# Norm ahead of the first layer's first FFN sweep, left half: four additions of squares on GpSimd instead of VectorE

## The chip, the cores and the metric

The kernel runs on one core of one Trainium2 chip. A core has a matrix engine (TensorE, PE in the rows; PEld are its weight loads), a vector engine (VectorE, DVE), an activation engine (ScalarE, ACT), a general engine (GpSimd, POOL), and a queue processor that only issues transfers here (SyncE, SP). Each engine executes its own list of instructions strictly in the order in which it was written out; instructions wait for other engines through semaphores. Transfers between device memory and the on-chip memory (SBUF) are carried by 16 DMA engines. The metric is the time of one execution in device microseconds (us), as the median of several runs.

## The reference, cut to what matters

The program is a diffusion backbone with two layers, 1024 channels, 1024 latent tokens and 256 context tokens. Layer 0 mixes tokens with a convolution, layer 1 with attention; behind each stands a SwiGLU feed-forward network (FFN). Around each part stand RMS norms. The part in question is the norm between the convolution and the FFN of layer 0:

```python
def rmsnorm(x, g):
    xf = x.astype(jnp.float32)
    y = xf * lax.rsqrt(jnp.mean(xf * xf, axis=-1, keepdims=True) + EPS)
    return (y * g.astype(jnp.float32)).astype(x.dtype)

x = x + g_x * rmsnorm(yx, norm_g[i, 1])
fx = rmsnorm(x, norm_g[i, 2]) * (1.0 + scf_x) + shf_x
x = x + gf_x * rmsnorm(swiglu(fx, ffn_w1[i], ffn_w3[i], ffn_w2[i]), norm_g[i, 3])
```

For `fx`, the squares of the new `x` have to be summed over all 1024 channels of a token before the first channel of that token can be scaled.

## The kernel before

**Layout.** Channels lie on the 128 partitions, so an activation is eight tiles `k = 0..7` of 128 channels by some number of tokens. The tokens are cut into three pieces: C (256 context tokens), L (the left 512 latent tokens) and R (the right 512). Each float32 operand of a matrix product is split into a rounded high part and the remainder, and each product is three matmuls: high by high, high by low, low by high (`mm3`, `mm3s`; L172 to L174 and L183 to L185, whose third has the weight's low part).

**Weights.** `wload` brings 512 KB of weights into one of two raw buffers (in the rows of the order `wr_73` and `wr_74`, in the profile `wr`) over SP's queue, ACT rounds it to `wh` (L144), and DVE subtracts to get `wl` (L148). SP may issue the next load into a raw buffer only when L148 has read it.

**The norm in question.** `post_pre` runs once for each piece. Its first part is `post`: for each tile DVE multiplies (L693) and adds the residual (L696), which gives the new `x` of the tile. Then `sink(k)` is called: `sq_acc` has ACT square the tile (L387 for the first, straight into the accumulator `acc`; L390 for the others, into one of four scratch buffers `sb`) and adds the square to `acc` (L391), and POOL issues the store of the tile to device memory (`x1d`, L710). Behind the eight tiles, `stat` has PE sum `acc` over the partitions (L365), DVE work out the reciprocal root in some 13 small instructions (L370, L343 to L351), and PE spread the result over the partitions (L379). Last, `apply` makes the FFN's input out of it, with a high part from ACT (L399 on DVE, then L404) and a low part from DVE (L405).

**What runs around it.** The pieces' `post_pre` for C and L is called, then `pw2` for R, which is the convolution's last product, and then the FFN's first sweep over C and L together (the second sweep is over R). R's `post_pre` is queued as background work of the first sweep; its first step has POOL issue four loads of 512 KB into the buffer `HR` (L685), which L's residual occupied before. The first weights of the sweep, `w1` and `w3` of `ft = 0`, are both needed at its first product, and C's products come ahead of L's.

**What sets the order.** The code is written as one program; a scheduler puts the instructions of each engine into a fixed order when the kernel is built, by its own estimate of when their inputs are ready and by the priorities that `later` gives. The order is fixed from then on, so an instruction whose input is late holds up everything behind it on its engine. Moving a few instructions can thereby change the order of others.

**Names in the rows.** `T_3535` is L's `x`, `T_3893` the FFN's input for C, `T_4028` and `T_4029` its high and low part for L, `T_3501` with `HS` the input of R's `pw2`. The profile leaves the numbers out.

Of the kernel before, what the change touches and what calls it, by code (L numbers as in the profile page):

```python
# [18 lines left out]
CTX = 256  # L19
# [27 lines left out]
def segs_of(c0, c1):  # L47
    out = []
    if c0 < CTX:
        out.append((0, min(c1, CTX) - c0, 1))  # L50
    if c1 > CTX:
        out.append((max(c0, CTX) - c0, c1 - c0, 0))
    return out


class Kern:
# [645 lines left out]
    def post_pre(self, l, y, yacc, xsrc, xdst, c0, c1, dcol, xtag, ftags, box):  # L702
        nc = self.nc
        n = c1 - c0
        segs = segs_of(c0, c1)
        acc = self.acc(n)

        def sink(k):
            self.sq_acc(acc, y[:, k, :], k)
            nc.gpsimd.dma_start(xdst[:, k, c0 - dcol:c1 - dcol], y[:, k, :])  # L710
        yield from self.post(l, 1, y, yacc, xsrc, c0, segs, sink, xtag)
        pb = self.stat(acc, n)
        yield self.pace
        hi, lo = self.halves(*ftags, n)
        box.append((hi, lo))
        for k in range(KT):
            self.apply(y[:, k, :], pb, l, 2, segs, hi, lo, k)
            yield self.pace
# [1005 lines left out]
```

## Time and profile before

| | |
|---|---|
| median of three runs | 2931.11 us (2930.49 to 2935.78) |
| profiled execution, its own time | 2934.98 us |
| its span, first to last instruction | 2933.2 us |
| mean granted TensorE clock | 0.987 |
| L's `post`, `stat` and `apply` on DVE | about 497 to 535 us of the span |
| DVE busy | 2160.1 us (74%) |
| ACT busy | 1334.4 us (45%) |
| POOL busy | 228.6 us (8%), 381 instructions |

An engine's busy time says nothing of where it was waited for; that is read from rows in order of time, in which the idle time ahead of an instruction stands at its end in brackets, with the instruction that ended it. A row with several instructions (x2, x3) gives the time from the first one's start to the last one's end. Rows of matmuls overlap, so the pace of PE is the distance between two starts.

### The profile page before, as it was taken

Reading aid. Unit: us, or ns where it says so; the run is one execution under the profiler, and the core shown is the slowest. Engines: PE = TensorE matmul, PEld = TensorE weight load, DVE = VectorE, ACT = ScalarE, POOL = GpSimd, SP = SyncE. Lnnn points to the kernel's source line nnn. Section 1 sums busy time; section 2 is a strip of 40 time slices with the busy share of each in tenths; the row PEclk is TensorE's granted clock in tenths of the full one; section 3 lists DMA queues with packets and bytes.
Section 4 is the critical chain, followed back from the end, with each engine's and each line's share of the span. In section 5 each row is a group of like instructions: output and inputs, shape, how many; then the busy total and the mean of one; then the engine's idle time right before and its main releaser. Section 6 shows DMA issues by size and latency. Waiting matters only on the chain.

```text
span 2933.2 us, 42735 instructions
## 1 busy us (share of the span) xinstructions
PE 2848.9 (97%) x16462; PEld 2446.5 (83%) x16462; DVE 2160.1 (74%) x3742; ACT 1334.4 (45%) x2229; POOL 228.6 (8%) x381
## 2 busy tenths in 40 slices
PE   8999989999999999999999999989999999999998
PEld 5888877888888889989888787767777778889997
DVE  6887788856556378877786899786666666786777
ACT  5212155432222245544444688645555543444444
POOL 0000001011022001000111111110000000010000
PEclk9999989999999999999999999999999999999999
DMA  6443443434356224333345211322222143353332
GB/s 249 133 127 99 111 136 137 139 116 148 104 171 209 64 78 167 108 103 111 119 160 166 89 46 46 101 83 81 65 74 83 60 151 97 109 171 102 105 97 77
DMA packets 131756, 336.58 MB, mean 115 GB/s; under 512 B 31329, under 2 KB 52865, under 8 KB 130657
## 3 DMA queue, kind: packets, MB, share of 16 engines
q1 hardware_dynamic: 78016, 222.33, 24.2%
q0 software_dynamic: 29344, 103.83, 10.8%
q10 hardware_dynamic: 24192, 7.70, 1.1%
q8 instruction: 129, 2.11, 0.3%
q14 instruction: 75, 0.61, 0.1%
HBM read 289.50 MB, written 38.93 MB: 112 GB/s over the span
## 4 chain that ended last, share of the span: by engine, by line
PE 86%; DVE 8%; issue 2%; ACT 2%; DMA 2%; ACTq 0%; SPq 0%; POOL 0%; DVEq 0%; POOLq 0%
PE ps L172 15%; PE ps L173 15%; PE ps L174 15%; PE ps L875 4%; PE ps L877 4%; PE ps L876 4%; PE ps L1116 4%; PE ps L1134 4%; PE ps L1140 2%; PE ps L1141 2%; PE ps L454 2%; PE ps L455 2%; PE ps L456 2%; PE ps L185 1%; PE ps L183 1%
## 5 line engine op out<-in xcount | busy, mean ns | idle before, releaser
L172 PE MATMUL ps<-T,wh 128*128 128x512 f32 (+1 forms) x1360 | 503.5, 371 | 0.6 <-DVE sm L839 0.4
L174 PE MATMUL ps<-T,wl 128*128 128x512 f32 (+1 forms) x1360 | 501.2, 369 | 2.0 <-DVE wl L148 2.0
L173 PE MATMUL ps<-T,wh 128*128 128x512 f32 (+1 forms) x1312 | 482.8, 368 | 0.0
L144 ACT CAST wh<-wr 128x1024 fp32r<-128x1024 f32 (+1 forms) x217 | 225.0, 1037 | 426.3 <-PE ps L173 311.2
L148 DVE TENSOR_TENSOR wl<-wr,wh 128x1024 fp32r<-128x1024 f32 (+1 forms) x217 | 261.9, 1207 | 174.7 <-ACT wh L144 173.4
L875 PE MATMUL ps<-T,wh 128*128 128x256 f32 x1092 | 310.5, 285 | 5.0 <-ACT wh L161 4.5
L876 PE MATMUL ps<-T,wh 128*128 128x256 f32 x1092 | 306.4, 281 | 0.0
L877 PE MATMUL ps<-T,wl 128*128 128x256 f32 x1092 | 305.4, 281 | 0.2 <-DVE wl L164 0.2
L1138 DVE TENSOR_TENSOR T<-ps,T 128x512 fp32r<-128x512 f32 x320 | 216.9, 687 | 108.4 <-ACT T L1137 107.7
L172 PEld LDWEIGHTS ps<-T,wh 128*128 128x128 f32 x1360 | 258.4, 190 | 43.1 <-ACT T L1506 1.7
L174 PEld LDWEIGHTS ps<-T,wl 128*128 128x128 f32 x1360 | 258.6, 190 | 42.5 <-DVE wl L148 2.2
L173 PEld LDWEIGHTS ps<-T,wh 128*128 128x128 f32 x1312 | 249.2, 190 | 37.7 <-DVE T L164 0.7
L1137 ACT CAST T<-ps 128x512 fp32r<-128x512 f32 x320 | 185.9, 585 | 191.5 <-PE ps L1134 177.6
L173 PE MATMUL ps<-HS,wh 128*128 128x512 f32 x656 | 257.9, 393 | 0.0
L172 PE MATMUL ps<-HS,wh 128*128 128x512 f32 x608 | 238.4, 392 | 0.9 <-ACT wh L144 0.9
L174 PE MATMUL ps<-HS,wl 128*128 128x512 f32 x608 | 237.4, 391 | 0.0
L875 PEld LDWEIGHTS ps<-T,wh 128*128 128x128 f32 x1092 | 206.1, 189 | 11.2 <-ACT wh L161 6.7
L876 PEld LDWEIGHTS ps<-T,wh 128*128 128x128 f32 x1092 | 206.6, 189 | 0.5
L877 PEld LDWEIGHTS ps<-T,wl 128*128 128x128 f32 x1092 | 206.1, 189 | 0.6 <-DVE wl L164 0.4
L1134 PE MATMUL ps<-cst,T 128*128 128x128 f32 x1100 | 189.5, 275 | 3.1 <-DVE T L1138 3.1
L1122 DVE TENSOR_SCALAR_CACHE_REDUCE T<-ps,rq 128x1280 f32<-128x1280 f32 x110 | 170.1, 1546 | 27.9 <-PE ps L1116 22.2
L1134 PEld LDWEIGHTS ps<-cst,T 128*128 128x128 f32 x1100 | 132.8, 141 | 49.2 <-DVE T L1138 30.2
(378 smaller groups left out, 6197.4 us busy)
## 6 DMA issues: line engine op xcount, KB each, us to landing
wr<-in_w SPq DMA_DIRECT2D x170, 512.0 KB, 3.6
wr<-in_pw SPq DMA_DIRECT2D x35, 512.0 KB, 3.5
HV<-in_wmodT POOLq DMA_DIRECT2D x56, 256.0 KB, 4.2
q<-in_wmodT POOLq DMA_DIRECT2D x56, 256.0 KB, 3.8
KB<-in_w SPq DMA_DIRECT2D x24, 512.0 KB, 3.6
HR<-in_w SPq DMA_DIRECT2D x23, 512.0 KB, 3.8
q<-in_w SPq DMA_DIRECT2D x23, 512.0 KB, 4.1
q<-qsd POOLq DMA_DIRECT2D x32, 256.0 KB, 3.4
```

The source lines that it names most:

```text
L144: nc.scalar.copy(hi, raw)
L148: nc.vector.tensor_tensor(lo, raw, hi.bitcast(F32), op=ALU.subtract)
L172: nc.tensor.matmul(out[:, :n], lhsT=wh, rhs=xh, start=k == 0, stop=False)
L173: nc.tensor.matmul(out[:, :n], lhsT=wh, rhs=xl, start=False, stop=False)
L174: nc.tensor.matmul(out[:, :n], lhsT=wl, rhs=xh, start=False, stop=k == nk - 1)
L875: nc.tensor.matmul(out, lhsT=wh, rhs=bh, start=first and k == 0, stop=False, **skip)
L876: nc.tensor.matmul(out, lhsT=wh, rhs=bl, start=False, stop=False, **skip)
L877: nc.tensor.matmul(out, lhsT=wl, rhs=bh, start=False, stop=k == 3, **skip)
L1122: nc.vector.tensor_scalar(out=pt, in0=sc, scalar1=rq[:, h:h + 1], scalar2=None, op0=ALU.mult, op1=ALU.min, accum_out=mn)
L1134: nc.tensor.transpose(tp[:, h * P:(h + 1) * P], Ps[h][:, j * P:(j + 1) * P], c["ident"])
L1137: nc.scalar.copy(ph, tp)
L1138: nc.vector.tensor_tensor(pl, tp, ph.bitcast(F32), op=ALU.subtract)
```

## The change

`post_pre` hands `sq_acc` an engine: for L (`c0 == CTX`) and tiles below 5 it is GpSimd. Tile 0 has no addition, so four are moved, those of tiles 1 to 4; the additions of tiles 5, 6 and 7 stay on DVE, and so do all seven of C and of R. Nothing else is edited.

```diff
         def sink(k):
-            self.sq_acc(acc, y[:, k, :], k)
+            self.sq_acc(acc, y[:, k, :], k, nc.gpsimd if c0 == CTX and k < 5 else None)
             nc.gpsimd.dma_start(xdst[:, k, c0 - dcol:c1 - dcol], y[:, k, :])
```

The scheduler's order changes with it. On DVE, this is the end of L's `post` before; `wr_73` holds the last weights of R's `pw2`, and `wr_74` the FFN's first `w1`:

```order
L693 SCALAR_TENSOR_TENSOR T_3535<-T_3535,col_2955,ps 128x512 x2
L391 TENSOR_TENSOR acc<-acc,sb 128x512
L696 TENSOR_TENSOR T_3535<-T_3535,HR 128x512 x2
L148 TENSOR_TENSOR wl<-wr_73,wh 128x1024
L391 TENSOR_TENSOR acc<-acc,sb 128x512
L148 TENSOR_TENSOR wl<-wr_74,wh 128x1024
L391 TENSOR_TENSOR acc<-acc,sb 128x512
L370 TENSOR_SCALAR nv<-ps 128x4
```

And this is the same place after the change, where the second `wr_73` is the FFN's first `w3`, and the second `wr_74` the `w1` of its next step:

```order
L693 SCALAR_TENSOR_TENSOR T_3535<-T_3535,col_2955,ps 128x512 x2
L696 TENSOR_TENSOR T_3535<-T_3535,HR 128x512 x2
L148 TENSOR_TENSOR wl<-wr_73,wh 128x1024
L148 TENSOR_TENSOR wl<-wr_74,wh 128x1024
L391 TENSOR_TENSOR acc<-acc,sb 128x512 x2
L148 TENSOR_TENSOR wl<-wr_73,wh 128x1024
L391 TENSOR_TENSOR acc<-acc,sb 128x512
L148 TENSOR_TENSOR wl<-wr_74,wh 128x1024
L370 TENSOR_SCALAR nv<-ps 128x4
```

Five additions stood ahead of the first L148 (the last of them is shown), now none does; and the two L148 of the next loads, which stood behind the first dozen instructions of the root, now stand ahead of L370.

On POOL, the difference at L's stores and the loads for R behind them (`ISA` sets GpSimd up for the additions and stood further back in the program before):

```order
-L710 DMA x1d<-T_3535 128x512 x8
+L710 DMA x1d<-T_3535 128x512 x2
+L391 ISA
+L391 TENSOR_TENSOR acc<-acc,sb 128x512
+L710 DMA x1d<-T_3535 128x512
+L391 TENSOR_TENSOR acc<-acc,sb 128x512
+L710 DMA x1d<-T_3535 128x512
+L391 TENSOR_TENSOR acc<-acc,sb 128x512
+L710 DMA x1d<-T_3535 128x512
+L391 TENSOR_TENSOR acc<-acc,sb 128x512
+L710 DMA x1d<-T_3535 128x512 x3
 L685 DMA HR<-in_xT 128x2x512 x4
```

The additions stand between the stores, and the four loads behind the last of either.

On PE, the difference among C's products of the first sweep, at the place where L379 stood:

```order
+L185 MATMUL ps<-T_3893,wl 128x256
 L184 MATMUL ps<-T_3893,wh 128x256
 L185 MATMUL ps<-T_3893,wl 128x256
-L379 MATMUL ps<-cst,nr 128x128 x4
+L183 MATMUL ps<-T_3893,wh 128x256
+L184 MATMUL ps<-T_3893,wh 128x256
+L365 MATMUL ps<-cst,acc 128x1 x4
 L185 MATMUL ps<-T_3893,wl 128x256
```

L365 moved back from among R's `pw2` to here, behind 11 of C's 48 products with the first `w1` and `w3`; L379 stands 25 of them further on, with the last 12 behind it. Ten products of C with the next `w1` now stand ahead of L's first low-part product, and all 22 products that are left of R's `pw2` stand ahead of C's first, of which two stood in front of them before.

## The prediction

> **What bounds the kernel now.** The page first. PE is busy for 97% of the span, so only time in which PE waits, or runs slowly, can be won:
>
> ```profile
> PE 2848.9 (97%) x16462; PEld 2446.5 (83%) x16462; DVE 2160.1 (74%) x3742; ACT 1334.4 (45%) x2229; POOL 228.6 (8%) x381
> PE 86%; DVE 8%; issue 2%; ACT 2%; DMA 2%; ACTq 0%; SPq 0%; POOL 0%; DVEq 0%; POOLq 0%
> ```
>
> Shares over the whole span don't say what four additions are worth, so the next view is PE in order of time where L's norm runs, about 497 to 541 us. PE waits there three times:
>
> ```profile
> 509.27 0.40 PE L173 MATMUL ps<-HS,wh 128*128 128x512 f32 x1
> 509.51 0.28 PE L183 MATMUL ps<-T,wh 128*128 128x256 f32 x1
> 509.63 0.28 PE L184 MATMUL ps<-T,wh 128*128 128x256 f32 x1
> 511.89 0.50 PE L174 MATMUL ps<-T,wl 128*128 128x512 f32 x1 [1.98 <-DVE wl L148]
> ...
> 526.54 0.50 PE L184 MATMUL ps<-T,wh 128*128 128x512 f32 x1 [0.36 <-DVE T L405]
> ...
> 540.33 1.05 PE L365 MATMUL ps<-cst,acc 128*128 128x1 f32 x8 [0.54 <-DVE acc L391]
> ```
>
> The distances of the starts also give PE's pace: 0.23 us for a product 512 wide, 0.12 for one 256 wide. The first wait has a second price, in the table by stretches (the eighth figure of a row, behind the five engines' busy times, is the granted clock):
>
> ```profile
> 510.00:512.00 2.00, 0.11 (x1) 0.11 (x2) 2.00 (x4) 1.23 (x2) 1.55 (x3) 1.00 0.25 98
> 512.00:516.00 4.00, 4.00 (x11) 3.14 (x12) 2.17 (x3) 0.22 (x1) 2.41 (x4) 0.57 0.94 297
> 516.00:520.00 4.00, 4.00 (x25) 3.46 (x24) 2.61 (x13) 0.83 (x1) 0.00 (x0) 1.00 1.01 387
> 540.00:545.00 5.00, 4.67 (x27) 4.14 (x28) 4.73 (x16) 0.79 (x2) 0.00 (x0) 1.00 0.46 116
> ```
>
> After the wait of 1.98 us PE has a clock of 0.57 for 4 us, which loses 4 x 0.43 = 1.7 us; after the wait of 0.54 it keeps 1.00. All that can be won here is 1.98 + 1.7 + 0.36 + 0.54 = 4.6 us, 0.16% of the time. A measurement of this kernel tells about 0.2%, 5.9 us, from no change.
>
> **DVE's side.** PE's first wait is for the first L148 of the order shown above. DVE in order of time, from the first addition on:
>
> ```profile
> 501.19 0.69 DVE L391 TENSOR_TENSOR acc<-acc,sb 128x512 f32<-128x512 f32 x1
> 501.79 1.29 DVE L696 TENSOR_TENSOR T<-T,HR 128x512 f32<-128x512 f32 x2
> ...
> 510.61 1.22 DVE L148 TENSOR_TENSOR wl<-wr,wh 128x1024 fp32r<-128x1024 f32 x1
> 511.75 0.68 DVE L391 TENSOR_TENSOR acc<-acc,sb 128x512 f32<-128x512 f32 x1
> 512.35 1.22 DVE L148 TENSOR_TENSOR wl<-wr,wh 128x1024 fp32r<-128x1024 f32 x1
> ...
> 517.09 0.16 DVE L370 TENSOR_SCALAR nv<-ps 128x4 f32<-128x4 f32 x1 [2.92 <-PE ps L365]
> ...
> 519.07 0.16 DVE L350 TENSOR_TENSOR nq<-nq,nh 128x4 f32<-128x4 f32 x1
> ...
> 522.62 1.22 DVE L148 TENSOR_TENSOR wl<-wr,wh 128x1024 fp32r<-128x1024 f32 x1 [2.17 <-ACT wh L144]
> 523.76 2.06 DVE L399 SCALAR_TENSOR_TENSOR sb<-T,col,ps 128x512 f32<-128x512 f32 x3
> 525.74 2.07 DVE L405 SCALAR_TENSOR_TENSOR T<-sb,mod,T 128x512 fp32r<-128x512 f32 x3
> ```
>
> From start to start an addition costs DVE 0.60 us (501.19 to 501.79) and an L148 1.14 (510.61 to 511.75). Five additions stand ahead of 510.61: 3.0 us, of which four go and the fifth moves behind.
>
> **What GpSimd takes, and takes back.** The trace has the same addition on POOL at another place, the norm of layer 1:
>
> ```profile
> 1432.63 1.22 DVE L148 TENSOR_TENSOR wl<-q,wh 128x1024 fp32r<-128x1024 f32 x1
> 1435.68 1.92 DVE L405 SCALAR_TENSOR_TENSOR T<-sb,mod,T 128x512 fp32r<-128x512 f32 x2
> 1439.47 1.34 DVE L405 SCALAR_TENSOR_TENSOR T<-sb,mod,T 128x512 fp32r<-128x512 f32 x1
> ...
> 1432.76 2.25 POOL L391 TENSOR_TENSOR acc<-acc,sb 128x512 f32<-128x512 f32 x1 [6.11 <-ACT sb L390]
> ...
> 1438.97 1.30 POOL L391 TENSOR_TENSOR acc<-acc,sb 128x512 f32<-128x512 f32 x1 [2.59 <-ACT sb L390]
> ```
>
> Undisturbed it takes 1.30 us. It doesn't run beside every DVE instruction: the one at 1432.76, started 0.13 us after an L148, takes 2.25, about what was left of the L148 more. And L405 at 1439.47, which takes 0.69 without POOL (2.07 for three), takes 1.34 beside the addition that began at 1438.97: it was held until about 1440.1, 1.1 us after the addition's start. L148 and L405 have two inputs in SBUF; so has L696, the residual's addition that DVE runs throughout L's `post`. L693, with one of its two from PSUM, I count as free of it, like L399, since all the lengthened rows are of the other kind. The Trainium skill, page "SBUF — State Buffer", section "Who interferes with whom", states this as a rule: a VectorE instruction with two SBUF inputs and a GpSimd instruction that reads SBUF exclude each other, and the one issued first keeps the other out to its end. It speaks against the change; by it nothing but the order of starts decides, and all four additions could hold VectorE in full.
>
> I follow the order through. L693 and L696 alternate in pairs, 1.32 and 1.20 us. The square of tile 1 is ready at 501.2, just as the second pair of L696 would start: a full hold of 1.1. The square of tile 2 comes while a pair of L693 runs, and its addition reaches 0.1 into the next L696. The third has a pair of L693 to itself: nothing. The fourth falls on the last pair of L696, or on the L148 behind it: 1.1. So the first L148 starts at 510.61 - 3.0 + 2.3 = 509.9 (bounds: 507.6 with no hold, 512.0 with four), and PE goes on at 511.2, not at 511.89. But the two products of C that filled 0.24 us of the wait now stand behind it: the gain is 0.45. PE's wait is then 1.7 us, near enough to 1.98 that I leave the slow clock as it is.
>
> **What moved with it.** The root (L370 to L351, 517.09 to 519.07 and two steps more without the L148 between: 2.35 us) now stands behind the L148 of the second `w1`, which waits for its cast and its load. ACT and POOL:
>
> ```profile
> 515.78 1.05 ACT L144 CAST wh<-wr 128x1024 fp32r<-128x1024 f32 x1 [4.36 <-DMA wr<-in_w]
> 521.54 1.05 ACT L144 CAST wh<-wr 128x1024 fp32r<-128x1024 f32 x1 [4.71 <-DMA wr<-in_w]
> ...
> 510.39 1.14 POOL L710 DMA_DIRECT2D x1d<-T  x2 [1.98 <-DVE T L696]
> 511.52 2.89 POOL L685 DMA_DIRECT2D HR<-in_xT  x4
> ...
> DMA to landing us min/median/max: 3.6/3.8/7.8
> ```
>
> The load of that `w1` was issued behind the L148 that ended at about 513.6 and landed at 521.5: 7.8 us, the longest in the last row (weight loads from 500 to 530 us), where 3.8 is usual, because the four loads of `HR` were issued from 511.52 on. After the change, the two L148 end at 511.1 and 512.2. POOL, whose fourth addition ends at about 509.4, still has three stores of 0.57 to issue and comes to its four loads at 511.0. So the `w1` is issued 1.2 us behind the first of them, and not 2.1. Its duration lies between 3.8 and 7.8; I take 6.0, from the middle, since it meets the same loads, but earlier: landed at 518.2. Cast 1.05, L148 1.14, root 2.35: the result is there at 522.8. PE comes to L379 at 511.2 + 22 x 0.23 + 1.7 + 11 x 0.12 + 0.8 (L365 and what lies around it) + 25 x 0.12 = 523.1. It doesn't wait. L399 starts about 0.75 later, at 523.6, as it did (523.76), so L's first low part is ready as early as before; PE has ten products with the second `w1`, 1.2 us, moved in ahead of it, so the wait of 0.36 goes. Those products of C are no gain in themselves: they are missing further on. L365 of R comes later in PE's order, behind nine products of 0.23 us, and DVE's additions for it don't move: the wait of 0.54 goes.
>
> Sum: 0.45 + 0.36 + 0.54 = 1.35 us. The profiled execution took 2934.98 us (span 2933.2, 1.8 around it) and would take 2933.6; it lies 3.9 us above the median of 2931.11, which becomes 2929.8. The rest of the program has the same instructions, some in another order, at R's `apply` and in the norm at 1430 us. PE's waits for additions of squares in the whole trace are small:
>
> ```profile
> PE ps L365 <- DVE acc L391: 2.5, 4, 0.8
> ```
>
> 0.54 of these 2.5 us is counted above; the others may move by some tenths either way, and I put nothing down for them.
>
> **The rivals.**
> - **Everything goes.** The holds are mild, PE's first wait falls below what makes the clock drop (between 0.54 and 1.98 us), and the `w1` lands before 518: 4.6 us won, 2926.5. For it: the holds are a matter of a tenth of a us in who starts first. Against it: it needs the mild case at both places. Chance 0.15.
> - **The wait moves to L379 (slower).** If the `w1` again takes 7.8 us, it lands at 520.0 and the root's result comes at 524.6, 1.5 us after PE, and the slow clock after it takes 1.7 once more. 3.2 less the 1.35: about 1.9 slower, 2933.0. It decides from a load of some 7 us on (result 1 us behind PE). For it: the same 3 MB of stores and loads crowd the queues after 511. Chance 0.3.
> - **Four full holds (slower).** The rule that only the order of starts counts, as worked out from the rows of layer 1: the first L148 starts at 512.0, and everything behind it, 1.4 us later than before, with the first wait lengthened by 1.4 + 0.24 and the load later as well: 2932 to 2935. Page "SBUF — State Buffer" of the Trainium skill gives the rule, and the two lengthened L405 agree with it. Against it: of the four squares, two come while L693 runs. Chance 0.1.
> - **The change doesn't do what it says:** the order shows four additions on POOL, so it does. None.
>
> **How the numbers follow.** The forecast has 0.45: 2929.8. All cases lie within 4.6 us below and 4 above 2931.1. The three runs of before scatter by 5 us, which a median of three can carry by 1 or 2. Range: 2926.0 to 2935.0. No case reaches 5.9 us by itself; 0.05 on either side is left for that scatter on top of the outer cases, and 0.9 for the same.
>
> **What would show it.** In the changed trace: L696 rows of 1.2 to 1.8 us beside POOL's additions (holds; if all stay at 0.69, the lock is wrong); PE's wait at the first L174 behind R's last `wl`, 1.7 us, with a clock near 0.57 after it; the cast of the second `w1` at about 518.2, and PE's wait at L379, near none or 1.5 us; no wait at L184 and at R's L365. A wait of several us at another place, behind an instruction that only the new order put there, would make the prediction wrong, and so would a clock that drops at further places.

## The result, and the profile after

| | before | after |
|---|---|---|
| median of 22 runs each, on one chip | 2934.12 us | 2929.34 us |
| ratio of the two, with its 95% interval | | 0.9985 (0.9979 to 0.9991) |
| profiled execution, its own time | 2934.98 us | 2928.56 us |
| its span | 2933.2 us | 2926.8 us |
| mean granted clock | 0.987 | 0.987 |

By the ratio the change gains 4.4 us, 2.6 to 6.2 by the interval. One of the 22 runs after took 3990.8 us at a clock of 0.651, and the ratio leaves it out. The time lies in the predicted range, near its middle. But the forecast was a gain of 1.35 us on a median of 2931.11; the runs of before that were made beside the changed ones have a median 3 us higher, and the gain measured is that of the rival "Everything goes", 4.6 us.

First the page again: the shares of the busy times, and the shares of the chain that ended last.

```profile
PE 2848.5 (97%) x16462; PEld 2446.9 (84%) x16462; DVE 2157.7 (74%) x3738; ACT 1335.1 (46%) x2229; POOL 238.8 (8%) x385
PE 87%; DVE 7%; issue 2%; ACT 2%; DMA 2%; POOL 0%; SPq 0%; DVEq 0%; ACTq 0%; POOLq 0%
```

DVE lost 2.4 us of work (four additions of 0.60), POOL gained 10.2: four additions that take 10 us together, where each would take 1.3 undisturbed. PE's busy time is only 0.4 us less. A slow clock counts as busy there (4.00 us of 4 at a clock of 0.57, in the prediction's table), so what was won has to be read stretch by stretch. The table (busy times of the five engines, then the clock, DMA's share and GB/s):

```profile
510.00:512.00 2.00, 2.00 (x11) 1.60 (x10) 1.51 (x3) 1.05 (x1) 2.00 (x5) 1.00 0.86 344
512.00:516.00 4.00, 4.00 (x33) 3.78 (x32) 3.61 (x9) 1.64 (x2) 2.79 (x4) 1.00 0.93 287
516.00:520.00 4.00, 4.00 (x35) 3.86 (x34) 2.85 (x10) 0.92 (x3) 0.00 (x0) 1.00 1.02 400
540.00:545.00 5.00, 5.00 (x37) 4.71 (x36) 3.34 (x6) 2.21 (x3) 1.02 (x2) 1.00 0.24 91
```

Where PE had 0.11 us of work in the first stretch and a clock of 0.57 in the second, it is now busy all the time at 1.00. None of its rows between 500 and 545 us has an idle time in brackets. The three waits and the slow clock are gone, and nothing came in their place up to 545 us.

The profiled executions differ by 6.4 us of span, more than that. Two places that both programs have tell how much of it is the change's, the first L693 of L and a wait of PE for a cast, 600 us later. First before, then after:

```profile
497.34 1.41 DVE L693 SCALAR_TENSOR_TENSOR T<-T,col,ps 128x512 f32<-128x512 f32 x2 [1.01 <-PE ps L379]
1104.36 0.39 PE L875 MATMUL ps<-T,wh 128*128 128x256 f32 x1 [0.45 <-ACT wh L161]
...
494.92 1.40 DVE L693 SCALAR_TENSOR_TENSOR T<-T,col,ps 128x512 f32<-128x512 f32 x2 [1.01 <-PE ps L379]
1097.73 0.39 PE L875 MATMUL ps<-T,wh 128*128 128x256 f32 x1 [0.45 <-ACT wh L161]
```

L693 is 2.42 us earlier after the change, ahead of the additions that moved. It starts anywhere from 494.08 to 497.87 in the traces of all these kernels, so I don't count that as the change's. From L693 to L875 it is 607.02 us before and 602.81 after: 4.2 us less, which agrees with the ratio. To compare a time of after with one of before, 2.4 is to be added to it.

DVE in order of time (start, duration, line, tiles; idle time ahead in brackets):

```profile
498.76 1.28 DVE L696 TENSOR_TENSOR T<-T,HR 128x512 f32<-128x512 f32 x2
...
501.29 1.28 DVE L696 TENSOR_TENSOR T<-T,HR 128x512 f32<-128x512 f32 x2
...
503.81 1.28 DVE L696 TENSOR_TENSOR T<-T,HR 128x512 f32<-128x512 f32 x2
505.01 2.35 DVE L148 TENSOR_TENSOR wl<-wr,wh 128x1024 fp32r<-128x1024 f32 x2
510.38 1.49 DVE L391 TENSOR_TENSOR acc<-acc,sb 128x512 f32<-128x512 f32 x2 [3.02 <-POOL acc L391]
511.79 1.22 DVE L148 TENSOR_TENSOR wl<-wr,wh 128x1024 fp32r<-128x1024 f32 x1
...
513.88 1.23 DVE L148 TENSOR_TENSOR wl<-wr,wh 128x1024 fp32r<-128x1024 f32 x1 [0.28 <-ACT wh L144]
```

Every pair of L696 takes 1.28 us, as it did: not one was held. The two L148 run at once behind them. What waits is DVE's fifth addition, 3.02 us for GpSimd's fourth, and PE doesn't wait for what stands behind it. GpSimd, which issues the stores and loads too:

```profile
498.72 2.49 POOL L391 TENSOR_TENSOR acc<-acc,sb 128x512 f32<-128x512 f32 x1 [0.34 <-ACT sb L390]
...
501.74 1.99 POOL L391 TENSOR_TENSOR acc<-acc,sb 128x512 f32<-128x512 f32 x1
...
504.25 4.26 POOL L391 TENSOR_TENSOR acc<-acc,sb 128x512 f32<-128x512 f32 x1
...
509.04 1.31 POOL L391 TENSOR_TENSOR acc<-acc,sb 128x512 f32<-128x512 f32 x1
...
511.90 2.89 POOL L685 DMA_DIRECT2D HR<-in_xT  x4
```

Take 1.3 us, the length of the fourth, from the end of each of the others, and its real start lies just ahead of the end of DVE's run: the first at 499.9, where the pair of 498.76 ends (500.0); the second at 502.4 (502.6); the third, which began in the middle of the pair of 503.81, at 507.2, behind that pair and both L148 (507.4). So by this reckoning the engine that was kept out is GpSimd, each time. And because its additions take that long, the four loads of `HR` are issued at 511.90, which is 514.3 in the time of before, 2.8 later than there. The weights' side of it, in ACT's casts, each of which waits for its load:

```profile
510.03 1.05 ACT L144 CAST wh<-wr 128x1024 fp32r<-128x1024 f32 x1 [0.85 <-DMA wr<-in_w]
512.80 1.05 ACT L144 CAST wh<-wr 128x1024 fp32r<-128x1024 f32 x1 [1.73 <-DMA wr<-in_w]
```

SP may issue the two weight loads when the two L148 are done, the second at 507.36, and the four loads of `HR` come 4.5 us behind that. The second `w1` is there 5.4 us after it could be issued (512.80), where it took 8.0 before; its cast, its L148 and the root follow, and L379 finds its input ready.

### The profile page after: what moved, and what is told of

Same layout as the page of the kernel before. It is cut to its first block, busy times and chain, and to the rows that moved or that the text cites. A ratio compares the mean times of both kernels' runs of the same rounds, so it can differ in the third digit from the quotient of the medians.

```text
span 2926.8 us, 42739 instructions
## 1 busy us (share of the span) xinstructions
PE 2848.5 (97%) x16462; PEld 2446.9 (84%) x16462; DVE 2157.7 (74%) x3738; ACT 1335.1 (46%) x2229; POOL 238.8 (8%) x385
## 4 chain that ended last, share of the span: by engine, by line
PE 87%; DVE 7%; issue 2%; ACT 2%; DMA 2%; POOL 0%; SPq 0%; DVEq 0%; ACTq 0%; POOLq 0%
PE ps L172 15%; PE ps L173 14%; PE ps L174 14%; PE ps L875 4%; PE ps L877 4%; PE ps L876 4%; PE ps L1116 4%; PE ps L1134 4%; PE ps L454 3%; PE ps L456 2%; PE ps L455 2%; PE ps L1140 2%; PE ps L1141 2%; PE ps L185 2%; PE ps L183 2%
## 5 line engine op out<-in xcount | busy, mean ns | idle before, releaser
L172 PE MATMUL ps<-T,wh 128*128 128x512 f32 (+1 forms) x1360 | 502.4, 370 | 0.5 <-DVE sm L839 0.4
L174 PE MATMUL ps<-T,wl 128*128 128x512 f32 (+1 forms) x1360 | 499.8, 368 | 0.0
L148 DVE TENSOR_TENSOR wl<-wr,wh 128x1024 fp32r<-128x1024 f32 (+1 forms) x217 | 261.8, 1207 | 169.4 <-ACT wh L144 168.1
L875 PE MATMUL ps<-T,wh 128*128 128x256 f32 x1092 | 310.7, 285 | 5.0 <-ACT wh L161 4.5
L174 PEld LDWEIGHTS ps<-T,wl 128*128 128x128 f32 x1360 | 257.7, 190 | 41.1 <-DVE wl L148 0.7
L174 PE MATMUL ps<-HS,wl 128*128 128x512 f32 x608 | 237.5, 391 | 0.0
L875 PEld LDWEIGHTS ps<-T,wh 128*128 128x128 f32 x1092 | 206.1, 189 | 11.2 <-ACT wh L161 6.7
```

Source lines behind the costliest of these rows:

```text
L148: nc.vector.tensor_tensor(lo, raw, hi.bitcast(F32), op=ALU.subtract)
L172: nc.tensor.matmul(out[:, :n], lhsT=wh, rhs=xh, start=k == 0, stop=False)
L174: nc.tensor.matmul(out[:, :n], lhsT=wl, rhs=xh, start=False, stop=k == nk - 1)
L875: nc.tensor.matmul(out, lhsT=wh, rhs=bh, start=first and k == 0, stop=False, **skip)
```

## The experiments

Four theories of where the gain came from, by name: **ENGINE**, VectorE has 2.4 us less to do at a place where PE waits for it; **ORDER**, the gain is the new order on VectorE, with both L148 ahead of the additions; **QUEUE**, the slow additions on GpSimd keep R's four loads back until the weight loads are through; and QUEUE with ORDER, which needs both. The first kernel is the change once more, beside the next two.

> The changed kernel once more, beside the others of this call. All theories: 3 to 6 us faster than before (4.4 us from the pairs so far), with no wait of PE between 490 and 545 us.

Measured: 2927.87 us where before has 2933.59, ratio 0.9982 (0.9973 to 0.9992). Its GpSimd additions take 2.49, 1.99, 4.26 and 1.31 us again, so the pattern isn't one execution's chance.

**The order alone.** All additions on VectorE, those of L with a later priority; the order that results has one addition ahead of the first L148 and six behind it.

```diff
-    def sq_acc(self, acc, src, k, eng=None):
+    def sq_acc(self, acc, src, k, eng=None, late=0):
...
-        (eng or nc.vector).tensor_tensor(acc, acc, sq, op=ALU.add)
+        with self.later(late): (eng or nc.vector).tensor_tensor(acc, acc, sq, op=ALU.add)
...
-            self.sq_acc(acc, y[:, k, :], k)
+            self.sq_acc(acc, y[:, k, :], k, late=40 if c0 == CTX else 0)
```

> All of L's additions stay on VectorE, but with a lower priority, so that the first two L148 come ahead of five of them; PE's order hardly differs from that of the changed kernel. ORDER (the gain comes from L148 being ahead of the additions, whoever does them): 3 to 5 us faster than before. ENGINE (VectorE has to be rid of four additions, 2.4 us): 2 us or less. QUEUE (the additions on GpSimd also pushed R's four loads behind the two weight loads; without them the loads come first again): no first wait, but the second w1 lands some 7 us after its issue, PE waits about 3 us at L379 and runs slowly after it: within 1 us of before.

Measured: 2931.59 us, ratio 0.9998 (0.999 to 1.0007). The rows of its profile: PE's waits, the L148 that lets the second `w1` be issued, the loads of `HR` and the cast of that `w1`. This execution is the slowest of the kernel's eleven (2941.33 us), but its excess lies behind the part in question: from L875 to the end of the span it has 1835.7 us, where before has 1828.8.

```profile
516.50 0.38 PE L183 MATMUL ps<-T,wh 128*128 128x256 f32 x1 [0.82 <-ACT wh L144]
517.76 0.39 PE L185 MATMUL ps<-T,wl 128*128 128x256 f32 x1 [0.40 <-DVE wl L148]
524.14 0.65 PE L379 MATMUL ps<-cst,nr 128*128 128x128 f32 x4 [1.63 <-DVE nr L351]
...
510.30 1.22 DVE L148 TENSOR_TENSOR wl<-wr,wh 128x1024 fp32r<-128x1024 f32 x1
...
508.87 2.88 POOL L685 DMA_DIRECT2D HR<-in_xT  x4
...
519.52 1.05 ACT L144 CAST wh<-wr 128x1024 fp32r<-128x1024 f32 x1 [3.07 <-DMA wr<-in_w]
```

The wait at L174 is gone, as with the change, so the order does what the prediction saw in it. But GpSimd, with no additions to make, issues the loads at 508.87, ahead of the second `w1`, which may be issued when that L148 ends at 511.52 and lands 8.0 us later. PE waits 2.85 us at three other places, 1.63 of it at L379: the mechanism of the prediction's slower rival, "The wait moves to L379". ORDER by itself falls.

**The order, and the loads held.** The same, with a copy on GpSimd, ahead of R's four loads, that reads L's finished `acc` and writes eight elements a row which the loads overwrite.

```diff
-        for q in range(0, m, 2):
-            load(q)
+        if i == 1 and c0 > CTX: nc.gpsimd.tensor_copy(xr[:, :, 0:1], self.accL[:, 0:m].unsqueeze(2))
+        for q in range(0, m, 2): load(q)
...
-        segs = segs_of(c0, c1)
-        acc = self.acc(n)
+        segs, acc = segs_of(c0, c1), self.acc(n)
+        self.accL = acc if c0 <= CTX else self.accL
```

> As late_adds, and R's four loads are held back by a copy of eight columns on GpSimd that needs L's finished sum of squares (it writes into R's buffer ahead of the loads, which overwrite it). ORDER: as late_adds, no difference between the two. QUEUE: 3 to 5 us faster than before, with the cast of the second w1 less than 6 us after the load's issue, and no wait at L379 above 1 us. ENGINE: as late_adds, 2 us or less.

Measured: 2928.74 us, ratio 0.9984 (0.9975 to 0.9992), the change's gain with no addition on GpSimd at all.

```profile
508.34 1.22 DVE L148 TENSOR_TENSOR wl<-wr,wh 128x1024 fp32r<-128x1024 f32 x1
...
515.11 2.89 POOL L685 DMA_DIRECT2D HR<-in_xT  x4 [0.34 <-POOL HR L686]
...
514.04 1.05 ACT L144 CAST wh<-wr 128x1024 fp32r<-128x1024 f32 x1 [1.39 <-DMA wr<-in_w]
```

The `w1` now lands 4.5 us after the L148 ahead of it (509.56), before the first load of `HR` is issued, and PE has no wait between 500 and 545 us. ENGINE falls here: VectorE does all the work that it did before.

**The loads held, in the old order.** The copy alone, without the later priority.

> The kernel before, all seven additions of L on VectorE in their old order; only R's four loads of `HR` are put behind a small GpSimd copy that reads L's finished `acc` (an extra copy of 8 elements a row, overwritten by the loads). QUEUE with ORDER (the gain needs both: the two L148 early, and the weight loads ahead of R's loads): the first wait of 1.98 us at L174 and the slow clock behind it stay; only the second `w1` comes earlier (cast at some 518.5 instead of 521.54), and PE's wait of 0.36 at L184 goes. About 0.4 us, 2933 where the kernel before has 2933.5, ratio 0.9995 to 1.0005. Rival, HOLD alone: the loads of `HR` were all that mattered, 3 to 4 us faster, 2930, and no wait at L174.

Measured: 2933.17 us, before 2933.76, ratio 0.9996 (0.9987 to 1.0005). First PE's waits and the clock behind the first one:

```profile
509.75 0.50 PE L174 MATMUL ps<-T,wl 128*128 128x512 f32 x1 [1.99 <-DVE wl L148]
518.56 0.65 PE L379 MATMUL ps<-cst,nr 128*128 128x128 f32 x4 [0.30 <-DVE nr L351]
...
510.00:512.00 2.00, 2.00 (x6) 1.57 (x6) 2.00 (x3) 0.00 (x0) 0.00 (x0) 0.53 0.82 258
512.00:516.00 4.00, 4.00 (x19) 3.31 (x19) 0.95 (x7) 1.05 (x1) 3.08 (x5) 0.81 0.94 288
```

The wait at L174 is back to 1.99 us, with 2 x 0.47 + 4 x 0.19 = 1.7 us of slow clock. Of the rest, the waits of 0.36 and 0.54 us are gone, and one of 0.30 at L379 is new. So the two halves are: the order removes the first wait, and the held loads keep a wait from coming up at L379. The run times of neither half alone can be told from before.

**One addition on GpSimd.** The diff is against the changed kernel. The order on VectorE comes out with both L148 early, as there.

```diff
-            self.sq_acc(acc, y[:, k, :], k, nc.gpsimd if c0 == CTX and k < 5 else None)
+            self.sq_acc(acc, y[:, k, :], k, nc.gpsimd if c0 == CTX and k < 2 else None)
```

> Only the addition of tile 1 goes to GpSimd (`k < 2`); the order that results on VectorE has a single other addition... ahead of the first L148, as in the change, and the remaining ones behind the second. QUEUE with ORDER: one slow addition of about 2.5 us on GpSimd is over by 501.2, so R's four loads come as soon as the last L696 is done, at about 507 to 508, level with or ahead of the two weight loads; PE waits 0.8 to 2 us at L183 and L379, and the time is that of the kernel before within 0.1% (2931 to 2934). Rival, ENGINE (VectorE rid of work at the critical place; the four additions behind the L148 cost nothing): as the change, 2929, 4 us faster than before.

Measured: 2932.76 us, ratio 0.9994 (0.9985 to 1.0003).

```profile
519.82 0.96 PE L379 MATMUL ps<-cst,nr 128*128 128x128 f32 x4 [3.20 <-DVE nr L351]
...
505.91 1.22 DVE L148 TENSOR_TENSOR wl<-wr,wh 128x1024 fp32r<-128x1024 f32 x1
...
505.08 2.88 POOL L685 DMA_DIRECT2D HR<-in_xT  x4
...
515.20 1.05 ACT L144 CAST wh<-wr 128x1024 fp32r<-128x1024 f32 x1 [4.69 <-DMA wr<-in_w]
```

One addition, though it takes 2.49 us, doesn't hold the loads at all: they are issued at 505.08, 0.83 us behind the end of the last pair of L696, where it is 0.84 with no addition on GpSimd (the order alone). The second `w1` lands 8.1 us behind its L148's end (507.13), and PE waits 3.20 us at L379.

**Four additions on GpSimd, but its queue free of stores.** The change with L's eight stores on SP's queue.

```diff
-            nc.gpsimd.dma_start(xdst[:, k, c0 - dcol:c1 - dcol], y[:, k, :])
+            (nc.sync if c0 == CTX else nc.gpsimd).dma_start(xdst[:, k, c0 - dcol:c1 - dcol], y[:, k, :])
```

> The changed kernel with L's eight stores to `x1d` on SyncE's queue; GpSimd issues its four additions with no store between them, so it comes to R's four loads of `HR` earlier. QUEUE: the loads are issued as soon as L's last L696 has freed `HR` and the fourth addition is over, at about the time of the two weight loads or ahead of them; the second `w1` lands late again, PE waits 1 to 3 us at L379, L183 or L174, and most of the gain is gone: 2931 to 2934, within 0.1% of the kernel before. Rival, ENGINE (four additions off VectorE are the gain): 2929 to 2930 as the change. The order on VectorE moves too: one addition stands ahead of the last pair of L696 and waits for GpSimd's fourth. On the lock, DMA (it is the store issued ahead of each addition that is kept out by VectorE's pairs, and the addition behind it): without stores the additions take 1.3 to 1.9 us and some L696 are lengthened by about 1.1. PAIRS (VectorE's next instruction goes first whatever GpSimd did before): they take 2 to 4 us again and no L696 is lengthened.

Measured: 2933.45 us, before 2933.37, ratio 0.9999 (0.999 to 1.0009).

```profile
509.86 0.50 PE L174 MATMUL ps<-T,wl 128*128 128x512 f32 x1 [2.09 <-DVE wl L148]
...
499.00 7.73 POOL L391 TENSOR_TENSOR acc<-acc,sb 128x512 f32<-128x512 f32 x4 [18.08 <-ACT sb L390]
508.96 2.88 POOL L685 DMA_DIRECT2D HR<-in_xT  x4 [2.23 <-DVE T L696]
...
510.00:512.00 2.00, 2.00 (x9) 1.65 (x10) 2.00 (x3) 0.00 (x0) 1.85 (x3) 1.00 0.78 204
512.00:516.00 4.00, 4.00 (x23) 3.35 (x22) 2.01 (x14) 1.05 (x1) 0.00 (x0) 1.00 1.00 398
```

The gain is gone with all four additions on GpSimd, against ENGINE again. It isn't a clean case for QUEUE: in this order VectorE has an addition ahead of its last pair of L696, waits 2.60 us there for GpSimd's fourth, and the wait at L174 comes from that. The loads (508.96) do stand ahead of the second `w1` again, which lands 7.6 us behind its L148. On the lock it says what was asked: without a store ahead of them the four additions take 7.73 us instead of 4 x 1.3, and every pair of L696 takes 1.28.

All kernels in one table. The load is the second `w1`, from the end of the L148 that lets it be issued to its cast; the waits are PE's between 500 and 545 us, with the time that a slow clock behind them cost. The distance from L693 to L875 is the one of the section on the result, in one trace of each kernel; it leaves out what differs ahead of this part and behind it.

| | R's loads issued, from that L148's end | the load takes | PE's waits, and slow clock | L693 to L875, against before | whole run, against before, by the ratio |
|---|---|---|---|---|---|
| before | 2.1 us ahead | 8.0 us | 2.88 + 1.7 | | |
| the change | 4.5 behind | 5.4 | none | -4.2 (again: -4.7) | -4.4 (-6.2 to -2.6) |
| order, loads held | 5.6 behind | 4.5 | none | -4.7 | -4.7 (-7.3 to -2.3) |
| order alone | 2.7 ahead | 8.0 | 2.85 + 0 | -1.1 | -0.6 (-2.9 to +2.1) |
| loads held alone | 1.2 behind | at most 5.9 | 2.29 + 1.7 | -1.3 | -1.2 (-3.8 to +1.5) |
| one addition | 2.1 ahead | 8.1 | 3.20 + 1.7 | -0.2 | -1.8 (-4.4 to +0.9) |
| no stores on GpSimd | 2.6 ahead | 7.6 | 3.87 + 0 | -0.6 | -0.3 (-2.9 to +2.6) |

Wherever R's loads are ahead, the `w1` takes 7.6 to 8.1 us, and where they are behind by 4 us and more, 4.5 to 5.4. The intervals of the whole run tell the two kernels without waits from no change, and nothing finer. The distance within a trace does: it follows what each kernel saved of before's 4.6 us of waits and slow clock, within 0.7 us. By it each half alone is worth 1.1 to 1.3 us and both together 4.7, in one trace each.

**The lock by itself.** Why was GpSimd kept out, and never VectorE? Five kernels of their own ask it; they compute nothing of the diffusion program. In the first, GpSimd meets twelve VectorE additions back to back; other parts have VectorE with an input in PSUM, or both due at once.

```python
for i in range(12):
    o = T("vb%d" % i)
    add(nc.vector, o, g, B)
    vs.append(o)
o2 = T("pb")
add(nc.gpsimd, o2, vs[2], B)
```

> The disputed hold by itself; nothing of the reference is computed, the input is copied to the output. Additions of 128x512 float32 on both engines. FIRST COME (whoever starts first keeps the other out until its instruction ends, one instruction at a time): a GpSimd addition that is due in the middle of twelve VectorE additions from SBUF takes about 1.3 + 0.6 us and holds the fourth or fifth of them for 1.1 us. ROW (VectorE's instructions back to back keep GpSimd out until the row ends): it takes 1.3 us more than what is left of the row, some 6 to 7 us, and no VectorE addition gets longer. With one VectorE input in PSUM both theories give 1.3 us and no hold. Where both are due at once: FIRST COME says either may win, ROW says nothing; where VectorE is due 0.3 us later, both say it is held to about 1.1 us after GpSimd's start.

GpSimd's addition that was due after the third of the twelve, then that due together with a single one of VectorE:

```profile
21.54 1.64 POOL L31 TENSOR_TENSOR pb<-vb,src 128x512 f32<-128x512 f32 x1 [2.65 <-DVE vb L31]
...
49.81 1.77 POOL L31 TENSOR_TENSOR pe<-ge,src 128x512 f32<-128x512 f32 x1 [4.55 <-ACT ge L35]
...
19.56 8.38 DVE L31 TENSOR_TENSOR vb<-gb,src 128x512 f32<-128x512 f32 x12 [5.96 <-ACT gb L35]
```

Alone it takes 1.26. Here it waits out the instruction that runs (1.64) and then holds the next: twelve VectorE additions take 8.38 us instead of 12 x 0.60 + 0.1 = 7.3. Beside additions with an input in PSUM neither is held. When both are due at once, VectorE goes first, three times out of three (1.77). That is FIRST COME, and not what the changed kernel shows.

The next two put the operands in place, a DMA issue ahead, 128x1024 instructions behind, and work on the other engines beside it.

> A kernel of its own (its output is only the copied input): eight trains on VectorE, all released by one copy on ScalarE, with one GpSimd addition released by the next copy, about 0.6 us later, in each. Trains a to d: ten additions from SBUF back to back (a: new outputs; b: in place; c: GpSimd in place too; d: GpSimd 0.4 us later); e, f: pairs of SBUF additions with pairs that read PSUM between them (f with a DMA issue ahead on GpSimd); g, h: four 128x1024 additions with fp32r output (h with the DMA issue). FIRST COME, as in the bench before: GpSimd waits out the VectorE instruction that runs, at most 0.7 us (1.1 in g and h), and then holds the next one: 1.3 to 2.4 us each. TRAIN (in the changed kernel GpSimd came in only where VectorE's run of SBUF pairs ended): some train, in place, fp32r or behind a DMA, keeps GpSimd out for two and more VectorE instructions, 2.5 us and up; which of them does tells what makes it so.

> A kernel of its own (its output is only the copied input): six trains on VectorE of SBUF pairs and PSUM pairs in place, each with one GpSimd addition in place released 0.6 us after the train: a alone; b with eight activations on ScalarE beside it; c with four loads of 512 KB from SyncE; d with four stores issued on GpSimd ahead of the addition; e with 40 matmuls on PE; f with two stores, the loads and the matmuls. FIRST COME: 1.3 to 1.9 us in all six, and one VectorE instruction held by about 1.1 us in each where GpSimd comes into SBUF pairs. If one of the backgrounds is what kept GpSimd out in the changed kernel, its train shows 2 us and more for the addition and no VectorE instruction held.

In all fourteen trains GpSimd came in at once or after one VectorE instruction: its additions took 1.27 to 1.81 us, with stores issued ahead, with loads, activations or matmuls beside them. FIRST COME again. The next copies the changed place instruction by instruction (squares of VectorE's own tiles, slices of one tile, two 128x1024 behind).

```python
for k in range(8):
    nc.vector.scalar_tensor_tensor(out=y[:, k, :], in0=y[:, k, :], scalar=col[:, k:k + 1], in1=ps,
                                   op0=ALU.mult, op1=ALU.mult)
    nc.vector.tensor_tensor(y[:, k, :], y[:, k, :], xr[:, k, :], op=ALU.add)
...
        nc.scalar.activation(sbs[k % 4], y[:, k, :], AF.Square)
        nc.gpsimd.tensor_tensor(acc, acc, sbs[k % 4], op=ALU.add)
    if store:
        nc.gpsimd.dma_start(d[:, k, :], y[:, k, :])
```

> A kernel of its own (its output is only the copied input) that copies the changed place: eight tiles as slices of one tile, L693 and L696 in pairs, squares on ScalarE, four additions on GpSimd in place, two 128x1024 instructions with fp32r output behind. Four rounds: without stores; with stores from GpSimd; with stores, 60 matmuls beside it, other addresses and the squares 0.35 us later; the same without stores and matmuls. FIRST COME (as in the three benches before): wherever GpSimd comes into a run of VectorE instructions from SBUF it waits out one of them and holds the next by about 1.1 us; VectorE's pairs of L696 take up to 2.4 us instead of 1.28. PAIRS (as in the changed kernel): the additions take 1.9 to 2.5 us beside a pair, some 4 us beside a pair with the two 128x1024 behind it, and every pair takes 1.28. If PAIRS shows here and not in the benches before, what sets them apart is in the form of the operands (slices of one tile, GpSimd's additions fed by squares of VectorE's own tiles) and not in the load of the other engines.

The second of its four rounds, GpSimd and then VectorE:

```profile
47.38 2.40 POOL L74 TENSOR_TENSOR acca<-acca,sb1a 128x512 f32<-128x512 f32 x1 [0.40 <-ACT sb1a L73]
50.30 1.99 POOL L74 TENSOR_TENSOR acca<-acca,sb2a 128x512 f32<-128x512 f32 x1
52.82 4.26 POOL L74 TENSOR_TENSOR acca<-acca,sb3a 128x512 f32<-128x512 f32 x1
57.61 1.27 POOL L74 TENSOR_TENSOR acca<-acca,sb0a 128x512 f32<-128x512 f32 x1
...
52.40 1.28 DVE L67 TENSOR_TENSOR ya<-ya,xra 128x512 f32<-128x512 f32 x2
53.61 2.35 DVE L78 TENSOR_TENSOR wla<-wra,ya 128x1024 fp32r<-128x1024 f32 x2
```

That is the pattern of the changed kernel (2.49, 1.99, 4.26, 1.31), the two in the middle to the hundredth, and no VectorE instruction held. The third and fourth round, with matmuls and without, with stores and without, show it too (4.25 and 4.71 for the third addition). So neither stores nor matmuls around these instructions are needed for it. But the instructions alone don't make it either: in the first round, whose second operand was still landing (its last pair waits 3.67 us for it), GpSimd came first twice, and a pair took 2.36 and 2.40 instead of 1.28. One more kernel asked whether it is the run's start (behind PSUM instructions without a gap, or from rest) or the operands.

> A kernel of its own (its output is only the copied input): eight trains on VectorE, one GpSimd addition due in the middle of each. Trains 1 and 2: eight SBUF additions from rest (different second operands; one second operand). 3 to 5: two instructions with an input in PSUM, then six SBUF additions without a gap (3, 4 as before; 5: GpSimd 0.3 us later). 6 and 7: PSUM pair, SBUF pair, PSUM pair, SBUF pair, GpSimd at two offsets. 8: four with PSUM, then four SBUF additions. START: what sets the changed kernel and its copy apart from the first three benches is that their run of SBUF instructions follows PSUM ones without a gap, where the benches began from rest; then GpSimd comes in after one instruction (1.3 to 1.9 us, one VectorE instruction held by 1.1) in trains 1 and 2, and only after the last SBUF instruction in 3 to 8 (up to 4 us, nothing held). OPERANDS: the benches read one and the same second operand throughout; then it is train 1 against train 2, and 3 against 4, that differ. Neither: all eight as in the first benches; it stays open.

A train of six behind two with PSUM, and one of four behind four; GpSimd first, then VectorE:

```profile
58.56 1.45 POOL L64 TENSOR_TENSOR acc<-acc,sq 128x512 f32<-128x512 f32 x1 [17.23 <-ACT sq L52]
...
135.69 2.46 POOL L64 TENSOR_TENSOR acc<-acc,sq 128x512 f32<-128x512 f32 x1 [15.31 <-ACT sq L52]
...
57.60 4.77 DVE L63 TENSOR_TENSOR y<-y,xr 128x512 f32<-128x512 f32 x6
...
134.53 2.49 DVE L63 TENSOR_TENSOR y<-y,xr 128x512 f32<-128x512 f32 x4
```

In the train of six GpSimd came in and held one (4.77 instead of 6 x 0.60 + 0.1 = 3.7); in that of four it stayed out to the end and held none (2.49). START and OPERANDS both fall, since trains 1 to 5 all let it in. What decides between the two behaviours stays open.

## Why the prediction was right and wrong

- **What bounds it, and how much is to be won:** right. PE's three waits and the slow clock behind the first are 4.6 us, and the change took all of them.
- **VectorE's 3.0 us ahead of the first L148:** right; five additions went from there.
- **The holds, 2.3 us:** wrong, and the step that failed. The prediction read from layer 1 that GpSimd and VectorE exclude each other, which holds, and then that whoever starts first goes first, and walked through the four additions by that. "So the first L148 starts at 510.61 - 3.0 + 2.3 = 509.9" was its sum. Here, each time, VectorE's whole run went first: GpSimd's third addition started at 504.25, ahead of the second L696 of its pair, and of both L148, and came behind all three. The prediction had named L696 at its usual length as the sign that the lock is wrong; the sign came, but the lock is there, and its other side paid for it. The first L148 started at 505.01, 507.4 in the time of before, at the end of the bounds that stood for no hold (507.6). The Trainium skill, page "SBUF — State Buffer", section "Who interferes with whom", gives issue order as what decides who blocks. The first bench agrees (a VectorE addition held by 1.1 us); this kernel and three rounds of its copy do not, if a row's start is taken for the issue.
- **The first wait shortened by 0.45, its slow clock kept (1.7):** wrong by the same step. With no hold there is no wait, and without a wait no slow clock: 3.2 us more than the forecast.
- **GpSimd comes to its loads at 511.0, the second `w1` takes 6.0 us and lands at 518.2:** wrong, by the same step's other side. What VectorE didn't lose GpSimd did: it came to its loads at 514.3 in the time of before. The load was issued 4.5 us ahead of them instead of 1.2 behind, took 5.4 and landed at 515.2.
- **No wait at L379, and those at L184 and at R's L365 gone:** right. But the wait at L379 was near: with both L148 early and the loads ahead, it is 1.63 and 3.20 us (order alone, one addition). Both have a load of 8 us, the change has one of 5.4 and no wait. That fits the rival's point of decision, some 7 us; no run with this order lies closer to it.
- **The time:** the forecast of 2929.8 stands beside a measured 2929.34, but that is a gain mis-sized by 3 us made up by a base that was 3 us higher, so its nearness is luck. By the ratio, "Everything goes", with a chance of 0.15, is what happened. The prediction took 5.9 us for the least that can be told from no change; with 22 runs each the interval is 1.8 us either way, so 4.4 can be told.

## What to carry to other kernels

Moving work to an idle engine also delays whatever that engine issues behind it, and here no gain that the run times can tell from nothing was left where that delay was missing: it put four 512 KB loads behind a weight load that PE needed first. Before such a move, look at what stands behind the moved work in the slower engine's queue, and at whose transfers it competes with; if the delay is what helps, a small dependence gives it without moving any work (2928.74 us here, with all additions on VectorE, five of L's seven behind both L148). And a load's duration depended here on what was issued just ahead of it (8.0 or 4.5 us), so price it from the order of issue, not from a median.

## What the runs showed of the hardware beyond that

- GpSimd's 128x512 addition takes 1.26 to 1.31 us alone. Beside a run of VectorE instructions that read two operands from SBUF it was kept out to the run's end in the kernel (up to 4.26 us) and in three rounds of its copy (up to 4.71), and for one instruction at most in all but one of the other trains (1.3 to 1.8, where it came in between two VectorE instructions the next was held by 1.1). Which of the two happens isn't explained.
- The clock doesn't follow from the length of a wait. Behind PE's wait at the same L174 it fell to 0.53 after 1.99 us in one kernel, and stayed at 1.00 after 2.09 us in another (loads held alone, no stores on GpSimd). The prediction's "between 0.54 and 1.98 us" as what makes it drop is therefore no threshold that the length alone gives.
- A 512 KB weight load took 4.5 us where four such loads of another queue were issued behind it, and 8.0 where they were issued ahead of it (the order on VectorE with the loads held, and without).
